# Prompt attention taken two heads at a time, with the value products of the pair issued by turns on the two column halves

## The chip, the cores and the metric

The kernel runs on one core of a Trainium2 chip. The metric is the time of one execution on the device, in microseconds; a kernel's time is the median of its runs. The engines that matter here are PE (TensorE, the matrix unit; its weight loads are shown as a second track, PEld), ACT (ScalarE), DVE (VectorE) and SP (SyncE, which issues most of the transfers).

## What is computed

One step of a two-layer encoder for two groups of streams: a prompt of 512 new positions, and 8 running streams with 16 new positions each on a cache of 512. Each layer runs three branches beside each other (latent attention, a wide convolution module, a short convolution), gates and merges them, and ends with an MLP. The part that the change touches is the prompt's attention, 8 heads with values 64 wide; cut to that, the reference is

```python
s = q_lat . ckv + q_rope . k_rope          # per head, 512 x 512
s = s * ATTN_SCALE
mask = (k_pos // 64) <= (q_pos // 64)      # block-causal
p = softmax(where(mask, s, -1e30))
o = p @ v                                  # v = ckv @ w_uv, 64 columns per head
```

## The kernel before

All data lie transposed, with features on partitions. Dense products split each fp32 operand into a high and a low part and add three products (line 437 high times high, 439 and 441 the mixed ones: `mm3_steps`). Weights come as 128x1024 blocks in one long stream: SP loads a block, ACT cuts off its high part (line 226), DVE its low part (line 227).

The prompt's attention is a loop of 32 steps per layer, one for each head h and block qt of 128 queries; the steps go through qt = 0 to 3 of one head, then of the next. PE's order there is the order of the code (the loop is in a stretch with a manual schedule for PE); ACT's and DVE's order is set by a scheduler that gives the attention's own operations priority. Three functions make up a step's work:

- `score(i)` (line 779): three products of 128 queries with the first 128(qt+1) keys (at least 256), into a PSUM tile `s`; then DVE sets the masked corner (786) and takes the row maximum (788), ACT takes the exponential and its sum (790), DVE the reciprocal (791) and scales (792). The result is the tile `p`.
- `turn_p(i)` (796): PE transposes `p` in blocks of 128 (801), and ACT copies them from PSUM to `pT` (803, four buffers).
- `value(i)` (807): qt+1 fp32 products `op<-pT,vt` (814), with 64 output partitions: head h uses partitions 64(h%2) to 64(h%2)+63 of the tile `op`, which two heads share. After the second head's last block ACT copies `op` to `oT` (816).

Step i of the loop (lines 850 to 863) issues `score(i + 2)`, then `value(i - 1)`, then a unit of other work, `turn_p(i)`, and two more units. The units come from `beside(i)`: mostly pieces of side projections (`side_tile`: three products of 128x320 each), in steps 2 to 4 of every eight pieces of the next pair's queries and keys (`heads_in`, 737), and from step 24 pieces of `absorb` (821). `heads_in` makes the two heads of a pair together. Its queries go to `qh` and `ql`, which have three buffers each, its keys to `kth[h % 3]` and `ktl[h % 3]`; the PSUM tiles of its products come from the pool `D0` with three buffers, as those of the side projections do.

After the loop comes the streams' attention, with loads of cached keys (`keys_of`, 875) that reuse the memory of the prompt's keys. At its end 16 value products of the same shape as line 814 are issued in one run (line 1005), in an order in which the output half `r0 = 64 * e` changes from one product to the next:

```python
for h_, ct, e in [(h_, ct, e) for h_ in range(0, NH, 2) for ct in range(2) for e in range(2)]:
```

Of the kernel before, what the change touches and what calls it, by code (L numbers as in the profile page):

```python
# [19 lines left out]
P = 128  # L20
# [44 lines left out]
SIDE = (("ca", 0), ("cg", 0), ("ca", 1), ("cg", 1), ("gc", 0), ("h", 0), ("gc", 1), ("h", 1), ("gb", 0), ("gb", 1))  # L65


KT2 = 2 * KT
NK = PAST + NQ

# [10 lines left out]
def block_groups(l):  # L81
# [14 lines left out]
    for i in range(-1, 4 * NH):  # L96
        if i % 8 == 2 and i < 24 or i < 0:
            g.append([("uqn", k, i // 8 + 1) for k in range(3)])
        for c in beside(i):
            if c == "s":  # L100
                if n % KT2 == 0:
                    g.append(sd[2 + n // KT2])
                n += 1
    g += sd[2 + -(-n // KT2):]
    for m in range(KT):
# [215 lines left out]
def trunk(tc, A, O):  # L321
    nc = tc.nc
# [76 lines left out]
    def mm_tile(name, n=HF, ps="D0"):  # L399
        b = banks[ps]  # L400
        return (b[0] if ps == "op" else b).tile([P, 512], F32, tag="mm", name=name)[:, :n]
# [42 lines left out]
    def mm3(*a, **k):  # L444
        for _ in mm3_steps(*a, **k):
            pass
# [61 lines left out]
    for l in range(DEPTH):  # L508
# [43 lines left out]
        vt = [pq.tile([P, 2, 512], F32, tag="kM", name=f"vt{i}", bufs=2) for i in range(2)]  # L552
# [175 lines left out]
        qt_h, mid, pv = {}, {}, {}  # L728
# [8 lines left out]
        def heads_in(pr):  # L737
# [34 lines left out]
            for c in range(2):  # L772
# [2 lines left out]
                    keys(ko)  # L775
                yield

        @first
        def score(i):
            h, qt = divmod(i, 4)  # L780
            qh, ql, kh, kl = qt_h[h]
            n = P * (qt + 1)
            s = mm_tile(f"s{l}_{h}_{qt}", 512, "s")
            qs, nk = slice(qt * P, (qt + 1) * P), max(n, 2 * P)
            mm3([s[:, :nk]], [(qh[:, qs], ql[:, qs])], [([kh[:, :nk]], [kl[:, :nk]])])
            nc.vector.memset(s[0:64, n - 64:n], -1e30)
            st = pp.tile([P, 4], F32, tag="st", name=f"st{l}_{h}_{qt}", bufs=6)
            nc.vector.tensor_reduce(out=st[:, 0:1], in_=s[:, :n], axis=AX.X, op=ALU.max, negate=True)
            pb = pp.tile([P, SEQ], F32, tag="p", name=f"p{l}_{h}_{qt}", bufs=4)
            nc.scalar.activation(out=pb[:, :n], in_=s[:, :n], func=AF.Exp, bias=st[:, 0:1], scale=1.0, accum_out=st[:, 1:2])  # L790
            nc.vector.reciprocal(out=st[:, 2:3], in_=st[:, 1:2])
            nc.vector.tensor_scalar(out=pb[:, :n], in0=pb[:, :n], scalar1=st[:, 2:3], scalar2=None, op0=ALU.mult)
            mid[i] = pb

        @first
        def turn_p(i):
            h, qt = divmod(i, 4)
            n, pb = P * (qt + 1), mid.pop(i)
            tp = psT.tile([P, 512], F32, tag="t", name=f"tp{l}_{h}_{qt}")
            for kt in range(qt + 1):  # L800
                nc.tensor.transpose(tp[:, kt * P:(kt + 1) * P], pb[:, kt * P:(kt + 1) * P], ident)
            pT = pp.tile([P, SEQ], F32, tag="pT", name=f"pT{l}_{h}_{qt}", bufs=4)
            nc.scalar.activation(out=pT[:, :n], in_=tp[:, :n], func=AF.Copy)
            pv[i] = pT

        @first
        def value(i):
            h, qt = divmod(i, 4)
            pT, pr, r0 = pv.pop(i), h // 2, 64 * (h % 2)
            if i % 8 == 0:  # L810
                pv["o"] = mm_tile(f"op{l}_{pr}", 512, "op")
            op = pv["o"]
            for kt in range(qt + 1):
                nc.tensor.matmul(op[r0:r0 + 64, qt * P:(qt + 1) * P], vt[kt // 2][:, kt % 2, h * 64:(h + 1) * 64], pT[:, kt * P:(kt + 1) * P], start=kt == 0, stop=kt == qt)  # L814
            if i % 8 == 7 and pr < 3:
                nc.scalar.activation(out=oT[:, pr, :SEQ], in_=op, func=AF.Copy)

        fill = side_units(range(2, 10))
# [24 lines left out]
        for i in range(2):  # L843
            for _ in range(2):
                next(fill)
            score(i)
# [3 lines left out]
        for i in range(4 * NH):  # L850
            if i % 8 == 2 and i < 24:
                nxt = heads_in(i // 8 + 1)
            if i == 22:
                next(ab)
            work = [{"h": nxt, "a": ab, "s": fill}[c] for c in beside(i)]
            if i + 2 < 4 * NH:
                score(i + 2)
            if i:
                value(i - 1)
            next(work[0], None)  # L860
            turn_p(i)
            for w in work[1:]:
                next(w, None)
        for _ in range(2):
            next(fill)
        value(4 * NH - 1)
        for _ in range(SF):
            next(fill)
# [5 lines left out]
        with pool(f"ps{l}", side="right") as ps:  # L874
# [126 lines left out]
            for h_, ct, e in [(h_, ct, e) for h_ in range(0, NH, 2) for ct in range(2) for e in range(2)]:  # L1001
                h = h_ + e
                r0 = 64 * e
# [226 lines left out]
        with pool(f"pf{l}", side="right") as pf:  # L1230
            nb = [0]
            hd = {}
# [222 lines left out]
def build(arrays):  # L1455
    nc = bacc.Bacc("TRN2", target_bir_lowering=False, num_devices=1)
    A = {k: nc.dram_tensor(f"in_{k}_dram", v.shape, mybir.dt.from_np(v.dtype), kind="ExternalInput").ap() for k, v in arrays.items()}
    O = {k: nc.dram_tensor(f"out_{k}_dram", s, F32, kind="ExternalOutput").ap() for k, s in OUTS.items()}
    with tile.TileContext(nc, schedule_with_timeline_sim=True) as tc:
        trunk(tc, A, O)  # L1460
    return nc
# [18 lines left out]
```

## Time and profile before

| | |
|---|---|
| median of 3 runs | 2011.75 us (2009.53 to 2013.53) |
| the profiled execution | 2013.47 us, of which the profile's span is 2011.6 us |
| PE busy | 1981.9 us, 99% of the span |
| PE weight loads (PEld) | 1908.5 us, 95% |
| DVE busy | 1343.5 us, 67% |
| ACT busy | 943.1 us, 47% |
| prompt's attention, layer 0 | 84 to 186 us of the span |
| prompt's attention, layer 1 | 1080 to 1181 us of the span |

The span starts with the first instruction and ends with the last; the time of an execution has some 2 us more. A busy PE is one that has a matmul in flight: matmuls are pipelined, so the time that one costs is the distance from its start to the start of the next, not its duration. In rows of the timeline the first number is the start, the second the length of the row, and "x8" says that eight instructions of one kind are merged in it. An fp32 product is shown as two instructions.

### The profile page before, as it was taken

What the parts mean: (1) busy time and instruction counts of PE and PEld (TensorE: products, weight loads), DVE (VectorE), ACT (ScalarE), POOL (GpSimd) and SP (SyncE); (2) the same over time, 40 slices, a digit from 0 to 9 for tenths busy, and PEclk for the clock granted to TensorE, in tenths of its full rate; (3) what the DMA queues carried; (4) which work ended last, traced back from release to release, by engine and by line L of the source; (5) the groups of instructions that cost most, each with busy time, mean ns of one, the idle gap of its engine ahead of it and who ended that gap; (6) DMA issues with size and microseconds to landing.
All of it is one profiled execution on the core that took longest, in us unless ns stands there. A gap on an engine that the chain in (4) does not pass through costs nothing.

```text
span 2011.6 us, 33112 instructions
## 1 busy us (share of the span) xinstructions
PE 1981.9 (99%) x13264; PEld 1908.5 (95%) x13264; DVE 1343.5 (67%) x2922; ACT 943.1 (47%) x1862; POOL 26.1 (1%) x47
## 2 busy tenths in 40 slices
PE   9999999999999999999999999999999999999997
PEld 9887899999999999999997878999999999999997
DVE  5764559867576656776777545697765776667675
ACT  5563322234464555446456532222454655553473
POOL 0000000000000000000000000000000000000000
PEclk9999999999999999999999989999999999999998
DMA  6113322213212333213341034222222223332242
GB/s 201 51 35 90 111 87 79 77 54 96 72 53 95 126 126 116 84 64 105 117 143 65 25 95 113 79 77 79 65 83 64 74 85 121 120 116 85 63 124 76
DMA packets 59882, 180.61 MB, mean 90 GB/s; under 512 B 10544, under 2 KB 13024, under 8 KB 59728
## 3 DMA queue, kind: packets, MB, share of 16 engines
q1 hardware_dynamic: 57472, 172.01, 27.3%
q0 software_dynamic: 2256, 6.48, 1.1%
q8 instruction: 104, 1.70, 0.4%
q14 instruction: 50, 0.41, 0.1%
HBM read 173.78 MB, written 4.69 MB: 89 GB/s over the span
## 4 chain that ended last, share of the span: by engine, by line
PE 94%; DMA 2%; ACT 2%; DVE 1%; issue 0%; SPq 0%; ACTq 0%; DVEq 0%
PE f L441 7%; PE f L439 7%; PE f L437 7%; PE mm_g L437 6%; PE mm_g L439 6%; PE mm_g L441 6%; PE op L814 2%; DMA raw<-in_W_dram 2%; PE mix L437 2%; PE mix L439 2%; PE mix L441 2%; PE C L437 2%; PE B L441 2%; PE C L441 2%; PE C L439 2%; PE B L437 2%
## 5 line engine op out<-in xcount | busy, mean ns | idle before, releaser
L226 ACT ACTIVATE wh<-raw 128x1024 fp32r<-128x1024 f32 (+3 forms) x170 | 166.6, 980 | 298.9 <-PE mm_g L439 201.2
L227 DVE TENSOR_TENSOR wl<-raw,wh 128x1024 fp32r<-128x1024 f32 (+3 forms) x170 | 191.0, 1124 | 123.8 <-ACT wh L226 123.4
L439 PE MATMUL f<-hl,wh 128*128 128x320 f32 x992 | 252.0, 309 | 0.0
L441 PE MATMUL f<-hh,wl 128*128 128x320 f32 x992 | 251.6, 309 | 0.0
L437 PE MATMUL f<-hh,wh 128*128 128x320 f32 x992 | 249.5, 309 | 0.0
L437 PE MATMUL mm_g<-xh,wh 128*128 128x320 f32 x768 | 181.9, 311 | 0.0
L441 PE MATMUL mm_g<-xh,wl 128*128 128x320 f32 x768 | 181.0, 309 | 0.0
L439 PE MATMUL mm_g<-xl,wh 128*128 128x320 f32 x768 | 180.5, 309 | 0.0
L439 PEld LDWEIGHTS f<-hl,wh 128*128 128x128 f32 x992 | 172.5, 188 | 0.0
L441 PEld LDWEIGHTS f<-hh,wl 128*128 128x128 f32 x992 | 172.4, 188 | 0.0
L437 PEld LDWEIGHTS f<-hh,wh 128*128 128x128 f32 x992 | 171.9, 188 | 0.0
L1058 DVE SCALAR_TENSOR_TENSOR cv<-U,vec,cv 128x320 f32<-128x320 f32 x360 | 133.9, 432 | 0.0
L437 PEld LDWEIGHTS mm_g<-xh,wh 128*128 128x128 f32 x768 | 129.7, 188 | 1.5 <-issue 0.3
L441 PEld LDWEIGHTS mm_g<-xh,wl 128*128 128x128 f32 x768 | 129.6, 188 | 0.2
L439 PEld LDWEIGHTS mm_g<-xl,wh 128*128 128x128 f32 x768 | 129.4, 188 | 0.3
L412 DVE TENSOR_TENSOR r<-r,f 128x320 f32<-128x320 f32 x192 | 85.4, 482 | 57.3 <-PE f L441 56.7
L226 ACT ACTIVATE wh<-sm 128x1024 fp32r<-128x1024 f32 x56 | 59.3, 1060 | 122.0 <-DVE sm L261 42.6
L227 DVE TENSOR_TENSOR wl<-sm,wh 128x1024 fp32r<-128x1024 f32 x56 | 68.4, 1222 | 49.1 <-PE C L441 28.8
L437 PE MATMUL mix<-mgh,wh 128*128 128x320 f32 x256 | 79.2, 311 | 0.0
L439 PE MATMUL mix<-mgl,wh 128*128 128x320 f32 x256 | 78.7, 309 | 0.0
L441 PE MATMUL mix<-mgh,wl 128*128 128x320 f32 x256 | 75.2, 309 | 0.0
L226 ACT ACTIVATE wh<-rx 128x1024 fp32r<-128x1024 f32 x28 | 29.6, 1059 | 88.7 <-PE f L439 76.9
(430 smaller groups left out, 5139.5 us busy)
## 6 DMA issues: line engine op xcount, KB each, us to landing
raw<-in_W_dram SPq DMA_DIRECT2D x204, 512.0 KB, 3.6
rx<-in_W_dram SPq DMA_DIRECT2D x28, 512.0 KB, 3.6
rxb<-in_W_dram SPq DMA_DIRECT2D x28, 512.0 KB, 3.7
kT<-in_ckvT_dram SPq DMA_DIRECT2D x16, 512.0 KB, 7.2
kM<-in_ckvM_dram SPq DMA_DIRECT2D x16, 512.0 KB, 4.5
raw<-in_W_dram SPq DMA_DIRECT2D x18, 384.0 KB, 3.0
raw<-in_W_dram SPq DMA_DIRECT2D x12, 256.0 KB, 2.7
x<-in_xT_dram SPq DMA_DIRECT2D x8, 320.0 KB, 5.8
```

The source lines that it names most:

```text
L226: nc.scalar.activation(out=wh[:, :n], in_=src, func=AF.Copy)
L227: nc.vector.tensor_tensor(out=wl[:, :n], in0=src, in1=R(wh[:, :n]), op=ALU.subtract)
L412: nc.vector.tensor_tensor(out=r[i][:, m, :], in0=r[i][:, m, :], in1=o, op=ALU.add)
L437: nc.tensor.matmul(o, wh, h[k], start=st, stop=False, skip_group_check=more)
L439: nc.tensor.matmul(o, wh, lo[k], start=False, stop=False, skip_group_check=more)
L441: nc.tensor.matmul(o, wl, h[k], start=False, stop=sp, skip_group_check=more)
L814: nc.tensor.matmul(op[r0:r0 + 64, qt * P:(qt + 1) * P], vt[kt // 2][:, kt % 2, h * 64:(h + 1) * 64], pT[:, kt * P:(kt + 1) * P], start=kt ...
L1058: nc.vector.scalar_tensor_tensor(out=o, in0=u, scalar=tap, in1=o, op0=ALU.mult, op1=ALU.add)
```

## The change

The steps of the attention are renumbered by a table: of every eight steps, which are now those of a pair of heads, the first head's blocks come at 0, 1, 3, 5, the second's at 2, 4, 6, 7. `value` does nothing in a step of the first head; in one of the second it issues the products of both heads for this block, by turns on the two halves of `op`. The loop, its units of other work and all buffers stay as they are.

```diff
+PAIR = ((0, 0), (0, 1), (1, 0), (0, 2), (1, 1), (0, 3), (1, 2), (1, 3))
...
+        def at_step(i):
+            e, qt = PAIR[i % 8]
+            return 2 * (i // 8) + e, qt
+
         @first
         def score(i):
-            h, qt = divmod(i, 4)
+            h, qt = at_step(i)
...
         def turn_p(i):
-            h, qt = divmod(i, 4)
+            h, qt = at_step(i)
...
-            pv[i] = pT
+            pv[h, qt] = pT
 
         @first
         def value(i):
-            h, qt = divmod(i, 4)
-            pT, pr, r0 = pv.pop(i), h // 2, 64 * (h % 2)
-            if i % 8 == 0:
+
+            h, qt = at_step(i)
+            if h % 2 == 0:
+                return
+            pr = h // 2
+            if qt == 0:
                 pv["o"] = mm_tile(f"op{l}_{pr}", 512, "op")
             op = pv["o"]
+            pTs = [pv.pop((2 * pr + e, qt)) for e in range(2)]
             for kt in range(qt + 1):
-                nc.tensor.matmul(op[r0:r0 + 64, qt * P:(qt + 1) * P], vt[kt // 2][:, kt % 2, h * 64:(h + 1) * 64], pT[:, kt * P:(kt + 1) * P], start=kt == 0, stop=kt == qt)
-            if i % 8 == 7 and pr < 3:
+                for e in range(2):
+                    hd = 2 * pr + e
+                    nc.tensor.matmul(op[64 * e:64 * e + 64, qt * P:(qt + 1) * P], vt[kt // 2][:, kt % 2, hd * 64:(hd + 1) * 64], pTs[e][:, kt * P:(kt + 1) * P], start=kt == 0, stop=kt == qt)
+            if qt == 3 and pr < 3:
                 nc.scalar.activation(out=oT[:, pr, :SEQ], in_=op, func=AF.Copy)
```

PE, layer 0, a step of head 1 before: the last score product, the value products of head 0's third block, a unit of the next pair's queries, and the transposes (`s_1_1` is head 1, block 1; a trailing number is a buffer).

```order
L441 MATMUL s_1_1_1144<-kth_909,ql_0_1_941 128x256
L814 MATMUL op_0_1085<-pT_0_2_1132,vt_209 64x128 x2
L814 MATMUL op_0_1085<-pT_0_2_1132,vt_210 64x128
L437 MATMUL uqn_1_1_1158<-qnh,wh_932 128x320
L439 MATMUL uqn_1_1_1158<-qnl,wh_932 128x320
L441 MATMUL uqn_1_1_1158<-qnh,wl_933 128x320
L801 MATMUL tp_0_3_1162<-ident,p_0_3_1081 128x128 x4
```

PE, layer 0, in the change (its line numbers are 2 to 12 higher): first a step in which no value product is issued, then the start of a step with those of both heads' second block.

```order
L443 MATMUL s_1_1_1099<-kth_909,ql_0_1_941 128x256
L439 MATMUL uqn_1_0_1120<-qnh,wh_932 128x320
L441 MATMUL uqn_1_0_1120<-qnl,wh_932 128x320
L443 MATMUL uqn_1_0_1120<-qnh,wl_933 128x320
L807 MATMUL tp_1_0_1124<-ident,p_1_0_1055 128x128
...
L443 MATMUL s_1_3_1200<-kth_909,ql_0_1_941 128x512
L826 MATMUL op_0_1149<-pT_0_1_1091,vt_209 64x128
L826 MATMUL op_0_1149<-pT_1_1_1189,vt_209 64x128
L826 MATMUL op_0_1149<-pT_0_1_1091,vt_209 64x128
L826 MATMUL op_0_1149<-pT_1_1_1189,vt_209 64x128
L439 MATMUL mm_ca_1_1_1070<-xh_100,wh_841 128x320
```

Every step had a group of value products between the scores and the first unit; now four of every eight have one, with products of two heads in turn.

ACT, layer 0, where the next pair's queries (`qh`) are written, before:

```order
L803 ACTIVATE pT_0_2_1132<-tp_0_2_1128 128x384
L750 ACTIVATE qh_1_0_1120<-uqn_1_0_1124 64x320
L761 ACTIVATE qh_1_1_1122<-qrhl 32x512
L750 ACTIVATE qh_1_1_1122<-uqn_1_0_1124 64x320
L790 ACTIVATE p_1_1_1151,st_1_1_1149<-s_1_1_1144,st_1_1_1149 128x256
L803 ACTIVATE pT_0_3_1167<-tp_0_3_1162 128x512
```

And in the change:

```order
L796 ACTIVATE p_1_1_1106,st_1_1_1104<-s_1_1_1099,st_1_1_1104 128x256
L752 ACTIVATE qh_1_0_1116<-uqn_1_0_1120 64x320
L763 ACTIVATE qh_1_1_1118<-qrhl 32x512
L752 ACTIVATE qh_1_1_1118<-uqn_1_0_1120 64x320
L809 ACTIVATE pT_0_2_1160<-tp_0_2_1156 128x384
L796 ACTIVATE p_0_3_1145,st_0_3_1143<-s_0_3_1138,st_0_3_1143 128x512
```

The second head's `qh` takes the buffer of head 0 of the pair at work. Head 0's last score, block 3, was issued a step before these rows; now it is issued right behind the unit that makes `uqn_1_0`.

## Rows read from the trace of the kernel before

**Rows 1.** The page: busy time, share of the span and instructions of each engine.

```profile
PE 1981.9 (99%) x13264; PEld 1908.5 (95%) x13264; DVE 1343.5 (67%) x2922; ACT 943.1 (47%) x1862; POOL 26.1 (1%) x47
```

**Rows 2.** Windows (stretch, its us; then busy us of PE, PEld, DVE, ACT, POOL; clock).

```profile
84.00:186.00 102.00, 101.61 (x622) 81.74 (x621) 56.27 (x174) 57.95 (x148) 2.00 (x3) 1.00 0.13 37
90.38:114.56 24.18, 24.18 (x153) 19.88 (x152) 14.25 (x44) 14.96 (x38) 0.00 (x0) 1.00 0.16 45
```

**Rows 3.** PE's waits in 84:186 and in 1080:1181: total us, times, longest.

```profile
PE s L439 <- DVE ktl L379: 0.3, 1, 0.3
...
PE s L437 <- DVE ktl L379: 1.9, 1, 1.9
```

**Rows 4.** Line 814, the value products: count, duration in ns, forms.

```profile
L814 PE MATMUL op<-pT,vt x320: 272/273/324, 90.4 to 1180.0; 128*64 128x128 f32 x160
```

**Rows 5.** PE's timeline around a group of one and a group of four products.

```profile
89.82 0.40 PE L439 MATMUL s<-ktl,qh 96*128 96x512 f32 x1
90.05 0.40 PE L441 MATMUL s<-kth,ql 96*128 96x512 f32 x1
90.38 0.43 PE L814 MATMUL op<-pT,vt 128*64 128x128 f32 x2
...
90.99 0.31 PE L439 MATMUL mm_ca<-xl,wh 128*128 128x320 f32 x1
...
110.76 0.34 PE L439 MATMUL s<-ktl,qh 96*128 96x384 f32 x1
110.93 0.34 PE L441 MATMUL s<-kth,ql 96*128 96x384 f32 x1
111.20 1.09 PE L814 MATMUL op<-pT,vt 128*64 128x128 f32 x8
...
112.47 0.31 PE L439 MATMUL mm_cg<-xl,wh 128*128 128x320 f32 x1
112.62 0.31 PE L441 MATMUL mm_cg<-xh,wl 128*128 128x320 f32 x1
```

**Rows 6.** PE's timeline around line 1005, 16 products by turns on the halves.

```profile
286.19 0.31 PE L437 MATMUL mm_g<-xh,wh 128*128 128x320 f32 x1
286.43 1.97 PE L1005 MATMUL uv<-olat,wuv 128*64 128x128 f32 x32
...
288.58 0.47 PE L439 MATMUL mm_g<-xl,wh 128*128 128x320 f32 x2
```

**Rows 7.** PE's timeline where a unit follows the scores with no value product.

```profile
85.08 0.28 PE L441 MATMUL s<-kth,ql 96*128 96x256 f32 x1
85.20 0.31 PE L437 MATMUL mm_ca<-xh,wh 128*128 128x320 f32 x1
85.35 0.31 PE L439 MATMUL mm_ca<-xl,wh 128*128 128x320 f32 x1
```

**Rows 8.** Timelines of DVE and PE: head 0's block 3 is scaled, then transposed.

```profile
93.05 0.49 DVE L792 TENSOR_SCALAR p<-p,st 128x512 f32<-128x512 f32 x1
...
96.98 0.60 PE L801 MATMUL tp<-ident,p 128*128 128x128 f32 x4
```

**Rows 9.** PE and ACT: head 1's block 3 is transposed and copied; a weight cut.

```profile
109.26 0.60 PE L801 MATMUL tp<-ident,p 128*128 128x128 f32 x4
...
109.96 0.60 ACT L803 ACTIVATE pT<-tp 128x512 f32<-128x512 f32 x1 [0.72 <-PE tp L801]
...
98.35 1.06 ACT L226 ACTIVATE wh<-raw 128x1024 fp32r<-128x1024 f32 x1
```

**Rows 10.** PE's longest wait behind the stage (186:290).

```profile
PE mm_gc L437 <- ACT gcs L591: 5.0, 1, 5.0
```

**Rows 11.** DVE: a row maximum over 512, low part of new queries, a copy.

```profile
90.93 0.68 DVE L788 TENSOR_REDUCE st<-s 128x1 f32<-128x512 f32 x1
...
95.85 0.48 DVE L751 SCALAR_TENSOR_TENSOR ql<-uqn,qh 64x320 fp32r<-64x320 f32 x1
...
96.69 0.42 DVE L762 CAST ql<-qrhl 32x512 fp32r<-32x512 f32 x1
```

## The prediction

> **What bounds the kernel now.** I read the page first, then one stage. The page shows PE busy for 1981.9 us of a span of 2011.6, 99%, with DVE at 67% and ACT at 47% [rows 1]. The reader should see that only PE's time counts, as long as the others keep up. That an engine is busy does not tell what one instruction costs, so the next view is the stretch of the attention: in layer 0 PE is busy for 101.61 of 102.00 us at full granted clock (1.00, which is 2.4 GHz), while DVE has 56.27 us of work and ACT 57.95 [rows 2]. PE's waits there are 0.3 us in layer 0 and 1.9 us in layer 1, both for the first keys [rows 3]. So in this stage a microsecond taken from PE's own stream is a microsecond of the kernel, until something else is late.
>
> **What the value products cost today.** There are 320 instructions of line 814 [rows 4], two for each of 160 products, 80 in a layer. Their duration of 273 ns is no price, since they overlap; I take distances between starts, in the timeline [rows 5]. For a group of one product, the last score product starts at 90.05 and the second product behind the group at 90.99, 0.94 us later. Without the group these two would be one score interval (90.05 - 89.82 = 0.23) and one interval of the side projection (112.62 - 112.47 = 0.15) apart, so the group costs 0.56 us. For a group of four products the same working gives 112.47 - 110.93 = 1.54, less 0.17 and 0.15: 1.22 us. Eight instructions instead of two cost 0.66 more: 0.11 us per instruction, and 0.34 us for having a group at all, which is lost around it. Where the scores are followed straight by a unit, the starts lie 0.12 and 0.15 apart [rows 7], the plain intervals: without a group, the 0.34 is not there. Groups of 1, 2, 3 and 4 products cost 0.56, 0.78, 1.00 and 1.22 us, 3.56 for a head, 28.5 for eight heads, **57.0 us in both layers**.
>
> **What they cost after it.** Removed: half of the groups, 16 of 32 in a layer. Changed: in the groups that stay, products of one half no longer follow each other. The nearest row is line 1005, with the same shape, in the same order of halves [rows 6]: 32 instructions lie between 286.19 and 288.58, 2.39 us, less two intervals of 0.15: 2.09 us. With 0.34 for the group, an instruction costs (2.09 - 0.34) / 32 = 0.055 us, half of 0.11. The new groups have 2, 4, 6 and 8 products: 0.34 + 4, 8, 12 and 16 times 0.055 are 0.56, 0.78, 1.00 and 1.22 us, 3.56 for a pair where there were 7.12. For four pairs and two layers that is 28.5 us, half of 57.0, so **28.5 us are saved**: 10.9 by groups that fall away (32 times 0.34), 17.6 by the halved instructions (320 times 0.055).
>
> Bounds of that price: were all of the 2.09 us charged per instruction (0.065) and 0.34 added to every group, a layer would cost 15.8 us instead of 14.2, and 25 us would be saved. At the other end a group that costs 0.065 an instruction and nothing else would save 36; the 0.34 in front of each of today's groups speaks against that. I take 28.5, as it follows from the row that has the same shape and order.
>
> **The rest of the change.** Score products, transposes, copies and units are the same in number and size, with other neighbours; DVE and ACT have the same work in a stage that is some 14 us shorter, 58 of 88 us at most. No DMA is added, and no weight block or load is asked for at another step; SP's and POOL's orders stay. What remains is who must now be on time:
> - The softmax. Today block 3 of head 0 has its scores from 89.58 on, the last of them ends at about 90.45 [rows 5], it is scaled by 93.54 and transposed from 96.98 [rows 8]: 3.4 us to spare. The tightest place in the new order is block 2 of head 0, scored in step 1 and transposed in step 3. Between them stand one group of 0.56 instead of three of 2.34 us, and one larger score (512 for 256 keys, 0.34 us more), so an estimate from these rows leaves 2 us. This costs nothing.
> - The copy to `pT`. Block 3 of head 1 is transposed from 109.26, copied by 110.56 and used at 111.20 [rows 5, 9]: 0.64 us spare. The score that stands between now has 256 instead of 384 keys, 3 times some 0.06 us less: 0.47 us spare. If ACT is in the middle of a weight cut of 1.06 us [rows 9], PE waits up to 0.6 us. I put down 0.1 us for each of eight pairs, 0.8 us.
> - The next pair's queries. Its second head writes the buffer of head 0, which is now read until the scores of step 3 are done. ACT waits there, and DVE's low part comes behind a corner, a maximum and a copy. The copy is 0.42, the corner, a smaller tile, at most as much: from those scores' end DVE needs up to 0.42 + 0.42 + 0.68 + 0.48 = 2.0 us [rows 11], while PE has the group (0.56), three units (0.44 each) and the score of step 4 (0.5) before it needs that PSUM tile: 2.4 us. It holds, with 0.4 us spare.
> - The copy of `op` has three steps instead of one before the tile is written again. The streams' first keys are loaded when the last score is done, and PE then gets to them some 0.3 us sooner, which adds up to 0.3 us of wait in each layer: 0.6 us.
>
> **The sum.** The profiled execution took 2013.47 us, 1.7 above the median: 2013.47 - 28.5 + 0.8 + 0.6 = 1986.4, and against the median of 2011.75 it is 1984.7. I forecast **1985 us**.
>
> **A rule that speaks against it.** The row of line 1005 shows 0.055 us by turns, against 0.11 within one half [rows 5, 6]: neighbours on different halves overlap. The Trainium skill (TensorE: Matmul & The Clock Gate, section Part 3, "What overlaps and what doesn't") says that a weight load overlaps with matmuls in flight only when its row group differs. Both halves here use all 128 rows, so by that rule the turns would bring nothing and the saving would be 10.9 us. The trace disagrees, in one run of 32 instructions; that is why the rule stays a rival.
>
> **Rivals.**
> - *The halves do not overlap here.* Line 1005 reads another operand and starts a new sum every second product; the value products add up to four in one place. If these cannot overlap, an instruction stays at 0.11 us and only 16 groups a layer go: 2011.75 - 10.9 = 2001 us. Against it: rows 6. The rule above would give this too. 0.06.
> - *The copies come late.* ACT is behind in many groups, not only in those of block 3: with 32 groups and 0.15 to 0.4 us each, 5 to 12 us come back: 1988 to 1997 us. For it: 0.47 us spare and weight cuts of 1.06. Against it: PE does not wait for `pT` once today [rows 3]. 0.14.
> - *Slower.* The second head's queries take the place of the value products as what PE waits for. ACT and DVE work through their queues in order; if the softmax of a later step stands behind the queries, and PE cannot reach the score that frees the buffer before that softmax, PE loses whole steps of 24.18 / 8 = 3.0 us [rows 2]. Six times this happens (three new pairs in each layer). Gain and loss are equal at 28.5 / 6 = 4.8 us each; two steps each make 2011.75 - 28.5 + 36 = 2019 us. Against it: the score in question is the next thing that PE issues. 0.03.
> - *The time is given back later.* PE waits 5.0 us behind the stage of layer 0, for a copy that stands behind a weight load [rows 10]. Were that load tied to something that does not move with PE, and its likes as well, the gain would turn into wait there: about 2011 us. Against it: those loads follow the stage's own last scores in SP's queue. 0.03.
>
> **How the numbers follow.** The forecast has 0.74: with the price's bounds and up to 3 us of small waits it reaches from 1981 to 1989. The late copies add 1989 to 1997 at 0.14. Both together hold 0.88, and leaving some room for a miss at their ends, **1981 to 1997** should hold the time 8 times in 10. A difference of 0.2%, 4 us, is about what a measurement of this kernel can tell from none. Faster by more: 0.74 + 0.14 + 0.06 = 0.94; within it: 0.03; slower: 0.03.
>
> **What would show it.** Right: 320 value instructions again, merged in rows of 4, 8, 12 and 16, those of 16 about 1.1 us long (0.27 + 15 times 0.055); the pairs' eight steps 20.6 us instead of 24.18; the stage of layer 0 some 14 us shorter at clock 1.00; no wait of PE for `pT`. Wrong: rows of 16 near 2 us (the halves do not overlap), waits of PE on ACT's line for `pT` or on the queries (late copies, or the slower case), or a shorter stage with a longer wait than 5.0 us behind it (given back).

## The result, and the profile after

The changed kernel takes **1989.09 us** (median of 4 runs, 1986.01 to 1991.92) where the kernel before, on the same chip, takes 2012.13 (4 runs, 2009.53 to 2013.53): ratio 0.9887, 95% interval 0.9867 to 0.9906, so 23 us faster. A second set of runs gave 1983.65 against 2008.91, ratio 0.9878 (0.9863 to 0.9894): 25 us. The forecast was 1985 us. The profiled executions took 1986.01 and 2013.47 us, 27.5 us apart, with spans of 1984.1 and 2011.6 us.

The page's first part for the kernel after, against [rows 1]:

```profile
PE 1959.4 (99%) x13264; PEld 1895.7 (96%) x13264; DVE 1341.9 (68%) x2922; ACT 939.5 (47%) x1862; POOL 26.1 (1%) x47
```

PE does the same 13264 instructions in 22.5 us less busy time and is still the bound at 99%. DVE and ACT have the work that they had. Line 814 is now line 826, and the three product lines 437, 439 and 441 are now 439, 441 and 443.

Windows of the kernel after (stretch, its us; then busy us and instructions of PE, PEld, DVE, ACT, POOL; granted clock). The first answers to the first of [rows 2]; the second is one pair of heads, from the first 512-key score to that of the next pair, and answers to the 24.18 us there; the third is the start of the stage in layer 1, and the fourth the same stretch in a second profiled execution of the same kernel (e1 below):

```profile
84.00:186.00 102.00, 100.58 (x676) 83.85 (x675) 62.53 (x190) 60.32 (x154) 3.44 (x5) 0.97 0.23 57
94.33:115.03 20.70, 20.70 (x153) 17.86 (x152) 13.73 (x42) 14.45 (x39) 0.00 (x0) 1.00 0.17 53
...
1068.00:1074.00 6.00, 6.00 (x34) 5.99 (x33) 2.26 (x12) 1.98 (x8) 0.00 (x0) 0.72 0.00 1
1068.00:1074.00 6.00, 6.00 (x44) 5.99 (x44) 2.99 (x14) 2.44 (x10) 0.00 (x0) 1.00 0.00 1
```

A pair takes 20.70 us with the same 153 instructions on PE (forecast 20.6), and PE is busy throughout. In the first stretch 676 instructions fit where there were 622; part of it now lies behind the stage.

PE's timeline around a group of four products for each head (start, us, engine, line, operation, out<-in, count; rows of one line in a row are merged), against [rows 5], and further up a step without a group:

```profile
88.90 0.28 PE L443 MATMUL s<-kth,ql 96*128 96x256 f32 x1
89.02 0.31 PE L439 MATMUL mm_ca<-xh,wh 128*128 128x320 f32 x1
...
108.39 0.28 PE L443 MATMUL s<-kth,ql 96*128 96x256 f32 x1
108.60 1.09 PE L826 MATMUL op<-pT,vt 128*64 128x128 f32 x16
109.62 0.41 PE L439 MATMUL mm_cg<-xh,wh 128*128 128x320 f32 x1
109.88 0.31 PE L441 MATMUL mm_cg<-xl,wh 128*128 128x320 f32 x1
```

Sixteen instructions take the 1.09 us that eight took, and by the working of the prediction the group costs 109.88 - 108.39 - 0.12 - 0.15 = 1.22 us, to the hundredth the forecast. The groups of 4, 8 and 12 instructions cost 0.56, 0.79 and 1.00. In a step without a group the unit follows the score after 0.12 us, with nothing lost.

PE's waits (us in total, times, longest): the first keys of layer 0 and of layer 1, against [rows 3], and the wait behind the stage in layer 0, against [rows 10]:

```profile
PE s L441 <- DVE ktl L381: 0.3, 1, 0.3
...
PE s L439 <- DVE ktl L381: 1.9, 1, 1.9
...
PE mm_gc L439 <- ACT gcs L593: 1.2, 1, 1.2
```

No wait for `pT` or for queries has come, and the 5.0 us behind the stage were 1.2 in this execution. In the second profiled execution of the same kernel (e1) that wait was 4.3 us, so it varies between executions.

**Where the time went.** I measure the stage from the start of its first score product to the end of its last group of value products, in the timeline of PE. The four rows that mark it in the kernel before, and then in the kernel after:

```profile
84.18 0.34 PE L437 MATMUL s<-kth,qh 96*128 96x256 f32 x1
...
183.78 1.09 PE L814 MATMUL op<-pT,vt 128*64 128x128 f32 x8
...
1080.45 0.38 PE L437 MATMUL s<-kth,qh 96*128 96x256 f32 x1 [1.92 <-DVE ktl L379]
...
1179.23 1.09 PE L814 MATMUL op<-pT,vt 128*64 128x128 f32 x8
```

```profile
85.22 0.34 PE L439 MATMUL s<-kth,qh 96*128 96x256 f32 x1
...
171.61 1.09 PE L826 MATMUL op<-pT,vt 128*64 128x128 f32 x16
...
1067.67 0.38 PE L439 MATMUL s<-kth,qh 96*128 96x256 f32 x1 [1.93 <-DVE ktl L381]
...
1154.72 1.09 PE L826 MATMUL op<-pT,vt 128*64 128x128 f32 x16
```

In layer 0 that is 171.61 + 1.09 - 85.22 = 87.48 us, in layer 1 1154.72 + 1.09 - 1067.67 = 88.14. In the kernel before it is 100.69 (84.18 to 184.87) and 99.87 (1080.45 to 1180.32). Together 175.62 against 200.56: **24.9 us** of the 27.5 lie in the two stages. The rest lies outside them, in waits and stretches of lower clock that differ between executions. Since those also lie between the medians, the table gives for every kernel the median with the kernel before measured beside it, and the two stages of the profiled execution, which are the cleaner measure of PE's stream. A star marks a stage whose start ran at a lower clock, which is explained below the table:

| kernel | median us | before, beside it | ratio (95%) | stages, us |
|---|---|---|---|---|
| before | | | 1 | 100.69 + 99.87 = 200.56 |
| the change, first set | 1989.09 | 2012.13 | 0.9887 (0.9867 to 0.9906) | 87.48 + 88.14* = 175.62 |
| the change, again (e1) | 1983.65 | 2008.91 | 0.9878 (0.9863 to 0.9894) | 87.47 + 86.62 = 174.09 |
| e2, no turns | 1988.71 | 2008.91 | 0.9907 (0.9891 to 0.9924) | 90.58 + 89.73 = 180.31 |
| e3, order of steps alone | 2006.53 | 2008.91 | 0.9991 (0.9983 to 1.0) | 100.77 + 101.43* = 202.20 |
| e4, scores beside the units | 1978.85 | 2008.91 | 0.9851 (0.9831 to 0.987) | 85.45 + 86.11* = 171.56 |
| e5, two groups a pair | 1980.31 | 2009.78 | 0.9855 (0.9839 to 0.9871) | 86.25 + 85.41 = 171.66 |
| e6, one group a pair | 1980.62 | 2009.78 | 0.9854 (0.9841 to 0.9868) | 85.42 + 84.59 = 170.01 |
| e7, one group, no turns | 1993.28 | 2009.78 | 0.9922 (0.991 to 0.9935) | 92.58 + 91.70 = 184.28 |
| e8, one group with e4's order | 1975.27 | 2009.78 | 0.9835 (0.9821 to 0.9848) | 82.98 + 83.66* = 166.64 |
| e9, turns of two products | 1987.45 | 2009.65 | 0.9886 (0.9872 to 0.9899) | 87.77 + 88.44* = 176.21 |
| e10, two groups with e4's order | 1977.25 | 2009.65 | 0.9835 (0.9819 to 0.9851) | 83.93 + 84.56* = 168.49 |
| e11, three tiles for `p` | 1983.74 | 2009.65 | 0.9868 (0.9854 to 0.9883) | 87.47 + 86.65 = 174.12 |

The stage of layer 1 in the first execution of the change (88.14) is 1.5 us longer than in e1 (86.62), with the same kernel. The third and fourth window above show why: behind the wait for the first keys the granted clock is 0.72 over 6 us, so part of that stretch ran at 1.2 instead of 2.4 GHz, and 34 instructions fit where e1 has 44 at a granted clock of 1.00. Over the first 6 us of that stage the granted clock is 0.72 in six of the thirteen profiled executions, those with a star, and 1.00 in the seven others; the steps up to the third score then take 4.1 instead of 2.6 us. The wait ahead of it is the same 1.9 us in all of them, and the one kernel that was profiled twice shows both. So a stage with a star is to be read as 1.5 us shorter when it is compared with one without, and layer 0, where no stage has such a stretch, can be compared as it stands. Read so, the two stages became 26.4 us shorter in the first execution of the change and 26.5 in e1.

### The profile page after: what moved, and what is told of

Same layout as the page of the kernel before. It is cut to its first block, busy times and chain, and to the rows that moved or that the text cites. A ratio compares the mean times of both kernels' runs of the same rounds, so it can differ in the third digit from the quotient of the medians.

```text
span 1984.1 us, 33112 instructions
## 1 busy us (share of the span) xinstructions
PE 1959.4 (99%) x13264; PEld 1895.7 (96%) x13264; DVE 1341.9 (68%) x2922; ACT 939.5 (47%) x1862; POOL 26.1 (1%) x47
## 4 chain that ended last, share of the span: by engine, by line
PE 93%; DMA 3%; ACT 2%; DVE 1%; issue 0%; SPq 0%; ACTq 0%; DVEq 0%
PE f L443 8%; PE f L441 8%; PE f L439 8%; PE mm_g L439 6%; PE mm_g L441 6%; PE mm_g L443 6%; DMA raw<-in_W_dram 2%; PE mix L439 2%; PE mix L441 2%; PE mix L443 2%; PE C L439 2%; PE B L439 2%; PE A L443 2%; PE C L441 2%; PE B L443 2%; PE A L439 2%
```

## The experiments

**Is the saving that of the turns, or that of the order?** Two kernels beside the change itself. e1 is the change again:

> The changed kernel as it is, to have its time against the kernel before with a narrower interval, and a second profile. If the prices of the prediction hold and nothing else moved, the medians are 26 to 28 us apart, as the two profiled executions are (2013.47 and 1986.01). If part of the gain is given back in most executions, by longer waits or more half-clock stretches behind the attention, they are 21 to 24 us apart, as the first medians were (2012.13 and 1989.09), while the eight steps of a pair take 20.7 us in the profile either way.

The medians are 25.3 us apart, between the two cases, and a pair takes 20.70 us: the stages hold the whole gain, and about 1 us of it does not show in the medians.

e2 keeps the pair of heads and the merged groups, and issues all products of the first head, then all of the second:

```diff
-            for kt in range(qt + 1):
-                for e in range(2):
+            for e in range(2):
+                for kt in range(qt + 1):
```

> The change with its two inner loops exchanged: in a group all products of the first head's half come first, then all of the second's. Groups, steps and buffers stay. If it is the turns that halve an instruction (0.11 to 0.055 us), 320 instructions cost up to 17.6 us more than in the change, less at most 1.8 us for the one change of halves that is left in each of 32 groups: 16 to 18 us slower than the change, 9 to 12 us faster than the kernel before, and eight steps of a pair take 22.7 to 22.9 us. If longer groups alone make the products cheap, it is as fast as the change, and the eight steps take 20.7 us.

e3 keeps the kernel before with its 32 groups a layer, each of one head, and takes only the order of the steps:

```diff
+PAIR = ((0, 0), (0, 1), (1, 0), (0, 2), (1, 1), (0, 3), (1, 2), (1, 3))
...
-            h, qt = divmod(i, 4)
+            h, qt = at_step(i)
```

> Only the new order of the steps: each step issues its own head's products again, as before. If the order itself costs and gives nothing, the time is that of the kernel before within 2 us, and eight steps take 24.1 to 24.2 us. If the order brings a wait (queries, softmax, copies), it is over 4 us slower than the kernel before and PE shows waits between 84 and 186 us; if the order is what gives, it is faster by 5 us or more.

The order of the steps alone is worth nothing that the profile would show as a gain: ratio 0.9991, eight steps in 24.21 us, and stages of 202.20 us, which are 200.7 without the 1.5 us of lower clock, against 200.56. But **e2 contradicts my theory**: without turns the kernel is only 5.1 us slower than with them, not 16 to 18, and eight steps take 21.49 us, not 22.7 to 22.9. Its timeline around the groups of two, three and four products for each head says where:

```profile
100.51 0.66 PE L826 MATMUL op<-pT,vt 128*64 128x128 f32 x8
...
105.26 0.28 PE L443 MATMUL s<-kth,ql 96*128 96x256 f32 x1
105.47 1.14 PE L826 MATMUL op<-pT,vt 128*64 128x128 f32 x12
...
106.80 0.31 PE L441 MATMUL mm_cg<-xl,wh 128*128 128x320 f32 x1
...
108.88 1.58 PE L826 MATMUL op<-pT,vt 128*64 128x128 f32 x16
```

The group of twelve costs 106.80 - 105.26 - 0.12 - 0.15 = 1.27 us; by turns it is 1.00. At 0.11 us an instruction it would be 0.34 + 12 times 0.11 = 1.66: some 0.4 us less is charged although no two products alternate. For sixteen the row is 0.49 longer than by turns, so 1.71 us, where 0.34 + 16 times 0.11 = 2.10 was due: 0.4 again. And the rows of 4 and 8 instructions are as long without turns (0.44 and 0.66 us) as with them.

**New theory.** The half price does not need turns; it is paid out at each *change of halves* inside a group. There the last products of one head and the first of the other run beside each other, up to some 0.4 us, about what four instructions (two products) cost by themselves at 0.11. Groups of one or two products a head get all of it from their one change; larger groups need more changes, and only there do the turns help: 0.27 + 0.49 = 0.76 us a pair, 6.1 us for eight pairs. The stages say the same: 180.31 - 174.09 = 6.2.

The trace also has the start of every single instruction, which the merged rows hide, and there the overlap is seen directly. In the change's group of twelve the starts come in twos: 105.638 and 105.645, 105.747 and 105.754, 105.856 and 105.863. From one two to the next it is 0.11 us, the interval of one half, so each half goes on at its own pace with the other beside it. In e2's group of twelve the second head's first instruction (its weight load waits for ACT, which copies `pT`) starts at 105.746, beside the third of the first head's six (105.740), and only from there on do the two run side by side. In the group of sixteen it starts at 109.370, beside the fifth of eight (109.364). In both it is the fourth from the end, so the overlap at a change reaches over some four instructions, two products.

**Does an order of the last pair matter?** In steps 24 to 31 of a layer each turn holds two absorb products (`qlat`, 64 rows) and one piece of a side projection. The change takes them as absorb, absorb, side; e4 puts the side piece first, so that the absorb products are neighbours:

```diff
-    return "aas" if 24 <= i < 32 else "sss"
+    return "saa" if 24 <= i < 32 else "sss"
```

> The change, and in the last eight steps of each layer the piece of a side projection is issued ahead of the two absorb products (64 rows of the array each) instead of behind them. In the profile of the change the scores are followed by such a product after 0.27 us where 0.18 is plain, and so the last pair's four steps without value products did not give back all of their 0.34 us: the layer's stage became 13.2 us shorter, not 14.2. If every change of the array's split costs 0.34 us there and back, each of 16 steps has one run of absorb products less: 3 to 5.4 us faster than the change. If the transposes between them cost the same split anyway, it is the same within 1 us.

It is 4.8 us faster than the change (1978.85 against 1983.65 on the same chip). Two steps without value products of the change, and then two of e4, in PE's timeline:

```profile
152.11 0.41 PE L439 MATMUL mm_h<-xh,wh 128*128 128x320 f32 x1
...
153.00 0.34 PE L443 MATMUL s<-kth,ql 96*128 96x384 f32 x1
153.27 0.49 PE L843 MATMUL qlat<-qsn,wukT 64*128 64x128 f32 x2
153.69 0.44 PE L807 MATMUL tp<-ident,p 128*128 128x128 f32 x2
154.06 0.48 PE L843 MATMUL qlat<-qsn,wukT 64*128 64x128 f32 x2
...
156.56 0.42 PE L439 MATMUL mm_h<-xh,wh 128*128 128x320 f32 x1
```

```profile
151.14 0.41 PE L439 MATMUL mm_h<-xh,wh 128*128 128x320 f32 x1
...
153.16 0.32 PE L439 MATMUL mm_h<-xh,wh 128*128 128x320 f32 x1
...
153.61 0.38 PE L807 MATMUL tp<-ident,p 128*128 128x128 f32 x2
153.92 0.71 PE L843 MATMUL qlat<-qsn,wukT 64*128 64x128 f32 x4
154.56 0.38 PE L439 MATMUL s<-kth,qh 96*128 96x256 f32 x1
...
155.01 0.31 PE L439 MATMUL mm_h<-xh,wh 128*128 128x320 f32 x1
```

The score product before `qlat` in the change is 0.27 us from it, where 0.18 is its plain interval, and each of the two groups of `qlat` pays such a switch; in e4 they are one group. The change's steps with scores over 384 and 256 keys (with two transposes and one) take 156.56 - 152.11 = 4.45 us together; e4's two with the same contents take 155.01 - 151.14 = 3.87. That is 0.29 a step. All eight turns of the last pair, those with value products too, make 87.47 - 85.45 = 2.02 us in layer 0, and as much in layer 1 once the 1.5 us of lower clock are taken from e4's 86.11. So some 4.0 of the 4.8 us lie in the stages; the other 0.8 I don't ascribe. The expectation asked for 3 to 5.4, with a saving in all 16 steps, and that is what came. This is also where most of the 1.0 us a layer that my forecast missed stayed: four of the groups that fell away stood in this last pair, next to an absorb product that pays the switch anyway.

**Fewer groups.** If a group costs 0.34 us for being there, merging further must pay. e5 issues the value products of blocks 0 and 1 together and of 2 and 3 together, e6 all of a pair at its end (with as many `pT` buffers as that needs, and three tiles for `p` to make room). The loop of e6:

```diff
-            if h % 2 == 0:
+            if h % 2 == 0 or qt not in (3,):
                 return
...
+            for q in range(qt + 1 - 4, qt + 1):
+                pTs = [pv.pop((2 * pr + e, q)) for e in range(2)]
+                for kt in range(q + 1):
+                    for e in range(2):
```

> The change, with two groups of value products for a pair instead of four: blocks 0 and 1 of both heads together, then blocks 2 and 3 (the copies in pT get a tile size by block, so that five of them can live at once in the same memory). The products and their turns stay. If a group costs 0.34 us whatever its length, 16 groups fewer save 5.4 us, about 1 us less in the last pairs, where absorb products follow the scores: 4 to 5.5 us faster than the change (1983.65 in the runs beside the first experiments). If the 0.34 us are paid again by what now stands next to each other, it is the same within 1 us.

> One group of 20 products for a pair, after its last step, with turns (eight copies live, and three tiles p instead of four, which makes the room). At 0.34 us a group, 24 groups fewer save 8.2 us, about 1.5 us less in the last pairs: 6 to 8.5 us faster than the change. If the three tiles p or the late copy of the last block make PE wait, it falls behind the variant with two groups.

e7 is e6 with all of one head's ten products ahead of the other's, so that only one change of halves is left in 40 instructions:

```diff
-            for q in range(qt + 1 - 4, qt + 1):
-                pTs = [pv.pop((2 * pr + e, q)) for e in range(2)]
-                for kt in range(q + 1):
-                    for e in range(2):
...
+            for e in range(2):
+                hd = 2 * pr + e
+                for q in range(qt + 1):
+                    pTs = {e: pv.pop((hd, q))}
+                    for kt in range(q + 1):
```

> The same one group, but the ten products of the first head first, then those of the second: one change of halves in 40 instructions. In the variant without turns, groups of 2 and 2 products were as fast as with turns (0.66 us), groups of 3 and 3 took 1.14 instead of 0.88 and groups of 4 and 4 took 1.58 instead of 1.09. Theory: around one change of halves about four instructions of the one half run beside four of the other, and that is worth some 0.34 us for each change, not more. Then this one takes 4.0 to 4.2 us a group instead of 2.2 to 2.4, and is 13 to 15 us slower than the one group with turns. Rival: products of both halves run beside each other wherever they stand in one group, up to some share. Then a group of 20 loses about as little as one of 8 lost (0.49 of 1.09 us, so 1.1 us of 2.4): 8 to 9 us slower.

The groups of e6 and then of e7, in PE's timeline:

```profile
105.83 0.28 PE L443 MATMUL s<-kth,ql 96*128 96x256 f32 x1
106.04 2.40 PE L827 MATMUL op<-pT,vt 128*64 128x128 f32 x40
...
108.63 0.31 PE L441 MATMUL mm_cg<-xl,wh 128*128 128x320 f32 x1
```

```profile
106.13 0.28 PE L443 MATMUL s<-kth,ql 96*128 96x256 f32 x1
106.34 4.20 PE L827 MATMUL op<-pT,vt 128*64 128x128 f32 x40
...
110.73 0.31 PE L441 MATMUL mm_cg<-xl,wh 128*128 128x320 f32 x1
```

With one change of halves 40 instructions cost 110.73 - 106.13 - 0.27 = 4.33 us, that is 0.34 + 40 times 0.11 less 0.41; with the products by turns 2.53 us, 0.055 an instruction and 0.33 for the group. The difference of 1.80 us times eight is 14.4, the stages differ by 14.27 and the medians by 12.7. So one change is worth 0.4 us in every group of two or more products a head, and the new theory holds at both ends. Here too the second head's first instruction starts beside the fourth from the end of the first head's twenty (108.146 and 108.140).

Merging paid less than the groups say. By the medians, each against the kernel before beside it, e5 is 4.2 us faster than the change, as expected, and e6 is 3.9 faster, not 6 to 8.5. In e5 two groups of 0.995 and 1.87 us stand for four that cost 3.56: 0.70 a pair, 5.6 in all; the stages are only 2.4 us shorter than e1's. In e6 it is 3.56 - 2.53 = 1.03 a pair, 8.2 in all, and 4.1 came. The next keys show what is late instead. PE's timeline at the first of them in layer 0, for the change:

```profile
97.61 0.34 PE L443 MATMUL s<-kth,ql 96*128 96x384 f32 x1
97.79 1.02 PE L775 MATMUL ko<-ckv,wuk 128*128 128x512 f32 x2
98.65 0.38 PE L807 MATMUL tp<-ident,p 128*128 128x128 f32 x2
```

and for e5, there and at the last of the layer:

```profile
96.18 0.34 PE L443 MATMUL s<-kth,ql 96*128 96x384 f32 x1
96.71 1.10 PE L775 MATMUL ko<-ckv,wuk 128*128 128x512 f32 x2 [0.19 <-DVE s L792]
97.64 0.38 PE L807 MATMUL tp<-ident,p 128*128 128x128 f32 x2
...
137.06 0.34 PE L443 MATMUL s<-kth,ql 96*128 96x384 f32 x1
137.47 1.10 PE L775 MATMUL ko<-ckv,wuk 128*128 128x512 f32 x2
```

Without the first small group PE reaches the keys' product 0.5 us earlier, and it starts 0.41 to 0.59 us behind the score, where in the change it is 0.17 to 0.18 at all six places. The trace names DVE's line 792, the masked corner, in two of three places of a layer, but `ko` has nothing to do with the corner. DVE's timeline there, in the change and then in e5:

```profile
96.99 0.49 DVE L753 SCALAR_TENSOR_TENSOR ql<-uqn,qh 64x320 fp32r<-64x320 f32 x1
```

```profile
96.07 0.49 DVE L753 SCALAR_TENSOR_TENSOR ql<-uqn,qh 64x320 fp32r<-64x320 f32 x1
96.60 0.11 DVE L792 MEMSET s<- 64x64 f32 x1
```

Ahead of the corner DVE ends the low part of the queries at 96.56, which reads `uqn`. Of the pool's three buffers an unfinished side projection holds one and the two `uqn` the others, so by the code `ko` is written to the buffer of the `uqn` that is read there, and that is the wait by all likelihood, put down to its neighbour: PE's sequencer has passed its wait on DVE at 96.65, before the corner ends at 96.71. In the change the low part ended at 97.48, PE came at 97.79 and did not wait. Over the six places the distance grew by 2.0 us, and 0.07 each behind it makes 2.4. With that, e5's 5.6 becomes 3.2; the 0.8 from there to the 2.4 measured is what four more groups in the last pairs would hold back at some 0.2 us each, next to absorb products. In e6 the same two items leave some 4.4 of the 8.2, and 4.1 came. A saved switch was turned into a wait.

e11 asks whether the third buffer of `p` that e6 gave up has a share in it:

```diff
-            pb = pp.tile([P, SEQ], F32, tag="p", name=f"p{l}_{h}_{qt}", bufs=4)
+            pb = pp.tile([P, SEQ], F32, tag="p", name=f"p{l}_{h}_{qt}", bufs=3)
```

> The change, with three buffers for the probabilities instead of four, as the kernels with one group have. If the lost buffer is what ate the missing 2 to 4 us of the one-group kernel, this kernel is 2 to 4 us slower than the change, with new idle time on the vector or scalar engine ahead of the exponentials. Rival: three buffers are enough, and it is the same as the change within 1.5 us.

It has not: 1983.74 us and stages of 174.12, as e1.

**Do the gains add up?** e8 is e6 with the order of e4, e10 is e5 with it.

> One group for a pair with turns, and the piece of a side projection ahead of the two absorb products in the last eight steps. If the two gains add (6 to 8.5 us from the groups, 4.8 us from the order of the pieces, and 1.5 us of the groups' cost that the last pairs had kept), it is 11 to 15 us faster than the change, near 1970 us; if both take the same loss away, it is 7 to 9 us faster.

> Two groups for each pair of heads, and the score step ahead of the two absorb steps that it shares a turn with in the last pairs. If the two edits add up: 4.2 us of the two groups and 4.8 us of the order, so 9 us below the change, as far as one group with that order went. Rival: the order only hides what larger groups hide too, and then it stands 4 to 6 us below the change.

(The "score step" of e10's expectation is the piece of a side projection; the edit is that of e4.) Both have a ratio of 0.9835, the lowest here, and can't be told apart. e8 has the lowest median, 1975.27 us, **34.5 us below the kernel before** and about 9 below the change, less than the 11 to 15 expected, since e6 lost its part to the keys; e10 is 32.4 below the kernel before and 7 below the change, where 9 was expected. In the stages the two edits more than add up: in layer 0 the order is worth 2.4 us with one group (85.42 to 82.98) and 2.3 with two (86.25 to 83.93), beside 2.0 with the four of the change. That fits what was expected: with this order the groups that fall away in the last pair no longer stand next to an absorb product. (The sums of the table show less, because e8 and e10 have a star.)

**What the change of halves needs.** e9 alternates by two products instead of one:

```diff
-            for kt in range(qt + 1):
+            for kk in range(0, qt + 1, 2):
                 for e in range(2):
...
+                    for kt in range(kk, min(kk + 2, qt + 1)):
```

> The change, with turns of two products: two for one head, two for the other, and so on. Theory A (about two products of one half run beside those of the other at each change of halves, worth some 0.34 us, so turns of two change halves often enough): the groups take the same time as with turns of one, at most 0.1 us more for the largest; the time is that of the change, within 1.5 us. Theory B (the overlap comes once in a group, where its only change of halves lies, or with turns of one product alone): the two largest groups take 1.14 and 1.58 us as without turns instead of 0.88 and 1.09, and the time is 5 to 6 us above the change.

Its rows of 12 and 16 instructions:

```profile
104.72 0.88 PE L827 MATMUL op<-pT,vt 128*64 128x128 f32 x12
...
107.85 1.14 PE L827 MATMUL op<-pT,vt 128*64 128x128 f32 x16
```

0.88 and 1.14 us; by turns of one they are 0.88 and 1.09, without turns 1.14 and 1.58. That is theory A: a group is as cheap, within 0.05 us, as long as no more than two products of a half stand in a row. The time is less clear than the rows: the ratio of 0.9886 lies between those of the two sets of the change (0.9887 and 0.9878), 1.6 us above the second, and the stages are 2.1 us longer than e1's, of which 1.5 are the stretch of lower clock in layer 1 and 0.6 the groups (a pair takes 20.77 us instead of 20.70).

## Why the prediction was right, and where its reasons were not

- **The total.** 1985 us was forecast, 1989.09 and 1983.65 were measured. The first is at the upper edge of what I gave the forecast itself (1981 to 1989), without the late copies that I had put beyond it. The stages, which the argument was about, became 24.9 and 26.5 us shorter in the two profiled executions, the first with 1.5 us of lower clock; the forecast was 28.5 less 1.4 of small losses, 27.1. That these come so close is in part luck: the 1.4 of losses did not come, and 2.0 of the 28.5 did not come either.
- **The price of a group** (0.34 us and 0.055 an instruction, from the row of line 1005) held to 0.01 us in all four sizes, and at 40 instructions as well (2.53, forecast by the same formula 2.54). The 0.34 does not lie in front of the group alone, as the paragraph on the bounds has it: the group of sixteen starts 0.21 us behind the score where 0.12 is plain, which is 0.09 of it, and the rest is lost at the group's first interval and behind it.
- **10.9 us by groups that fall away** held where a score and a unit of 128 rows now meet (0.12 us, no loss). It failed in the four such places of a layer's last pair, where an absorb product pays the switch instead: about 0.2 us each, 0.85 a layer. With 0.05 in each of the other three pairs (24.21 to 20.70 us, 3.51 instead of 3.56) that is why layer 0 gained 13.2 us and not 14.2.
- **17.6 us by the halved instructions** is the step whose size was right, as it came from a row with the same order, and whose reason was too narrow. I put all of it down to the turns ("products of one half no longer follow each other"). e2 shows that turns are worth 6 of it and that some 11.4 come from having both heads in one group, with one change of halves: 0.22, 0.42, 0.39 and 0.39 us in the four groups of a pair, times eight. Row and formula couldn't tell the two apart, since [rows 6] alternate and [rows 5] have no change of halves at all.
- **The small losses** (0.8 us for late `pT`, 0.6 for the first keys) did not come: no wait for `pT` is listed, and the waits for the first keys are 0.3 and 1.9 us as before.
- **The rivals.** *The halves do not overlap* is refuted by e7 beside e6: the same work with one change of halves instead of turns costs 13 us more (14 in the stages). The starts in twos show the overlap itself. *Copies come late*, *slower by the queries*: PE waits for neither. *Given back later*: the wait behind the stage was 1.2 and 4.3 us, not longer than 5.0. But in e5 and e6, which go one step further, giving back did begin, at the keys' product. The prediction had that place: its item on the next pair's queries left 0.4 us there, and the 0.56 of the first small group was part of it (0.3 were left in the change, 97.48 to 97.79). e5 and e6 take this group away, and I did not do that sum again before I expected their gains.

## What to carry to other kernels

Where two heads or tiles write the two column halves, bring their products into one group before thinking of a fine interleave: each change of halves is worth up to 0.4 us here, and with no more than two products of a half in a row nearly all of it is had. Count the places where PE goes from full-width products to half-size ones and back (0.2 to 0.34 us each) as an expense of its own, and put half-size products of different stages beside each other. After each gain look for the next engine's release at the point that PE now reaches earlier, and redo the sums of spare time with what is gone: here the next 0.4 us a pair became a wait on DVE. And when single profiles are compared, compare the granted clock of the same stretch first: 1.5 us of lower clock hid more than a third of what e4 gains in the stages.

## What was not expected

- A run of products on one half, followed by a run on the other, does not always cost more than alternating: groups of 2 + 2 products take 0.66 us either way, 3 + 3 take 1.14 against 0.88, 4 + 4 take 1.58 against 1.09, and 10 + 10 take 4.20 against 2.40.
- Half the rows count like half the columns: the absorb products with 64 rows pay a switch for each of their groups, and two neighbouring groups pay it once, which gave 0.25 us a step on the mean of eight.
- The granted clock was 0.72 over the first 6 us of layer 1's stage in one execution of the change and 1.00 in the other, and 0.72 in five and 1.00 in six of the other profiled kernels, all with the same wait of 1.9 us ahead of it. What decides it stays open; no run here tries it.
